# Attention of a two-layer encoder trunk rearranged: value projections, the value product, the rotation, the root vector and the order of the projections

## The chip, the cores and the metric

The kernel runs on one core of a Trainium2 chip, in one launch. The metric is the device time of that core in microseconds (us). A measurement of this kernel can tell about 0.2% from no change, which is 2.3 us here.

## What is computed

The input x is 512 tokens by 1024 features, in float32. Each of two layers does the following:

```python
h = rmsnorm(x, attn_norm[l])
proj = h @ w_in[l]                        # 1024 -> 3072: sb_q, sb_k, sb_v, df_q, df_k, df_v, 512 columns each
# stick-breaking group: 8 heads of 64, causal and strict
z = q @ k.T / 8
w = exp(log_sigmoid(z) + sum of log_sigmoid(-z) over the keys between), 0 where key >= query
sb_out = w @ v
# differential group: 4 heads with two score maps of 64 and values of 128
dq, dk = rope(df_q), rope(df_k)
p = softmax(dq @ dk.T / 8)                # a query sees the keys of its own and of earlier chunks of 64 tokens
df_out = rmsnorm((p[0] - lam * p[1]) @ dv, subln_norm[l]) * (1 - lambda_init)
x = x + concat(sb_out, df_out) @ w_o[l]
# dense part
x = x + square(relu(rmsnorm(x, mlp_norm[l]) @ w_ff1[l])) @ w_ff2[l]
```

After the second layer comes a last rmsnorm. The result is float32.

## The kernel before

**Number format.** A float32 product is made of three TensorE products. Each operand is split into a high part (`hi`, rounded by ScalarE as it copies into the format fp32r) and the rest (`lo`, a VectorE subtraction). `three` (L278) issues hi*hi, hi*lo and lo*hi into the same PSUM bank; they are lines L281, L282 and L283 of the profile. Weights are split in the kernel too: `_Weights` (L86) loads a raw block of 128 x 1024 by a transfer of SyncE's queue (L99), and splits it on ScalarE (L116, tile `whi`) and VectorE (L117, tile `wlo`). A block is split when the block before it starts to be used, so its split has about one block of TensorE work to be done in.

**Projections.** x is held with features on the 128 partitions and the 512 tokens along the free axis. A projection block (`block`, L291) is 128 columns of w_in: the weights are the stationary operand, h is the moving one, eight chunks of features by three products of 512 columns, 24 matmuls. Its result has the projected columns on the partitions. The root of the norm differs from token to token. It is not yet known when the first blocks run, so h leaves it out, and it is multiplied in at the eviction: `rms_a` (L244) transposes the sums of squares, reduces them and raises them to -1/2 on GpSimd (L259, tile `rcol`, a token on each partition). From this it makes two diagonal matrices (L264, L266), and `rms_b` (L271) multiplies them with a matrix of ones, which spreads the roots along the free axis of every partition (tile `rbc`). The same pair of functions does the norm of each differential head (tiles `rs_d`, `dgh`, `dgl`, `rb_d`).

**Evictions.** A value block (`evict_v`, L367) is multiplied by `rbc` on VectorE (L369), then turned by four TensorE transposes (L374, tile `vT`), since the value product needs keys on the partitions, and then split (L381 on ScalarE, L382 on VectorE). A differential query or key block (`evict_d`, L430) is multiplied by cosine and by sine on VectorE (L433, L434). GpSimd then forms the two sums of the rotation (L441, L442), 3.5 us of the planner's clock later the result is split, and twelve transfers (L408) on SyncE's queue lay it out in the stacks `st` and `kl` from which the scores are made.

**Attention.** A unit is half of the queries (256) of one head. Three stages run at a lag: scores and weights (`s1_df` L488, `s1_sb` L468), transposes of the weights in 128 x 128 pieces (`s2` L542, transposes at L555, split at L224 and L225 into `zh`, `zl`, `fh`, `fl`), and the value product (`s3` L572, matmuls at L583 and L584 for stick-breaking heads and at L281 to L283 for differential ones, bank `O`). For the first half of the queries `s3` multiplies two key blocks, for the second half four, all of 256 columns, with a strip of zeros where a key block is later than the queries. That is six matmuls of 256 columns for each kind of product and head. There are two kinds of product for a stick-breaking head, three for a differential one.

**Order of the work.** TensorE takes its instructions in program order. `dense` (L698) walks `ORDER` (L31): d is a pair of differential query and key blocks, w a differential value block, s and u the same for stick-breaking heads. Then comes the first half of the output projection, `wo(1)`. After each matmul triple of this, the planner adds attention steps, at a rate that spreads the attention's planned cost (`ATT`) over the planned dense time (`DENSE`), all but the last `TAIL` of it. A unit may start when the planned clock says that its stacks are laid out. The second half, `wo(0)`, follows, and then the dense part of the layer. The framework then orders each engine's instructions by its own estimate of when they can start.

**PSUM.** Eight banks: two "t" (transposes), two "mm" (projections), three "s" (scores), one "o" (value product). A block can start when its bank has been evicted.

Of the kernel before, what the change touches and what calls it, by code (L numbers as in the profile page):

```python
# [9 lines left out]
F32 = mybir.dt.float32  # L10
# [7 lines left out]
P = 128  # L18
S = 512
# [15 lines left out]
RST = 2  # L35
WARM = 10
RA, RB, DLY_V = (21, 20), (32, 31), 3.5
# [3 lines left out]
TAIL, ATT, DENSE, CAP = 6.0, 54.0, 145.0, 0.1  # L41
# [8 lines left out]
def _unit_list():  # L50
# [5 lines left out]
    for l in range(L):  # L56
        for item in ORDER:
            b = int(item[1])
            if item[0] == "d":
                units.append(("x", l, b, 0))  # L60
                units.append(("x", l, b, 1))
            elif item[0] == "s":
                qk(l, SBQ, SBK, b)
            else:
                units.append(("p", l, (SBV if item[0] == "u" else DFV) + b * P))
# [86 lines left out]
def trunk(ctx, tc, xT, w, w2, gains, gfin, lamv, cos, sin, out):  # L152
# [23 lines left out]
    rbc = cp.tile([P, S], F32, tag="rbc", name="rbc")  # L176
# [19 lines left out]
    ones = cp.tile([P, 1], F32, tag="ones", name="ones")  # L196
    nc.vector.memset(ones, 1.0)
# [18 lines left out]
    chi = cp.tile([P, 4], F32R, tag="chi", name="chi")  # L216
    clo = cp.tile([P, 4], F32, tag="clo", name="clo")
    ones_r = cp.tile([P, 1], F32R, tag="onesr", name="ones_r")
    nc.vector.memset(ones_r.bitcast(F32), 1.0)
    fin = cp.tile([P, 24], F32, tag="fin", name="fin")  # L220
    cp.tile([P, 88], F32, tag="trail", name="trail")
# [22 lines left out]
    def rms_a(src, inv_n, col, name, eng, dgt, floor=None):  # L244
        pt = bank("t", "rs_" + name)
        if RST and eng is not nc.gpsimd or RST == 2:
            for j in range(4):
                nc.tensor.transpose(pt[:, j * P : (j + 1) * P], src[:, j * P : (j + 1) * P], ident)
            nc.vector.tensor_reduce(out=ms, in_=pt.rearrange("p (j f) -> p j f", j=4), axis=AX.X, op=ALU.add)
            if floor is None:  # L250
                nc.vector.tensor_scalar(out=ms, in0=ms, scalar1=inv_n, scalar2=EPS, op0=ALU.mult, op1=ALU.add)
            else:
                nc.vector.scalar_tensor_tensor(
                    out=ms, in0=ms, scalar=inv_n, in1=floor, op0=ALU.mult, op1=ALU.add)
        else:
            for j in range(4):
                nc.tensor.matmul(pt[:, j : j + 1], src[:, j * P : (j + 1) * P], ones, start=True, stop=True)
            nc.vector.tensor_scalar(out=ms, in0=pt[:, 0:4], scalar1=inv_n, scalar2=EPS, op0=ALU.mult, op1=ALU.add)
# [3 lines left out]
        dg_hi, dg_lo = dgt("dgh" + name), dgt("dgl" + name)  # L262
        idb = ident.unsqueeze(1).to_broadcast([P, 4, P])
        eng.tensor_mul(  # L264
            dg_hi.rearrange("p (j t) -> p j t", j=4), idb, chi.bitcast(F32).unsqueeze(2).to_broadcast([P, 4, P]))
        eng.tensor_mul(  # L266
            dg_lo.rearrange("p (j t) -> p j t", j=4), idb, clo.unsqueeze(2).to_broadcast([P, 4, P]))

        return dg_hi, dg_lo
# [47 lines left out]
    for l in range(L):  # L317
        with ExitStack() as actx:
# [9 lines left out]
            zt = []  # L328
            for i in range(2):
                zh = ap_.tile([P, 512], F32R, tag=f"zh{i}", name=f"zh{l}_{i}")  # L330
# [779 lines left out]
```

## Time and profile before

| | |
|---|---|
| median of 3 runs | 1173.92 us (1173.44 to 1175.14) |
| the profiled execution: its span, first to last instruction | 1173.7 us |
| TensorE busy, matmuls | 1149.1 us, 98% of the span, 5454 matmuls |
| VectorE busy | 817.8 us, 70% |
| ScalarE busy | 651.7 us, 56% |
| GpSimd busy | 213.7 us, 18% |
| transfers | 170.11 MB, mean 145 GB/s |

No separate time is given for the profiled execution; its span lies 0.2 us under the median of the runs. The page names the engine, the line of the kernel, the operation and the tiles (`out<-in`). A matmul's recorded duration overlaps the next one, so what a matmul costs is read from the distance of two starts, in a timeline of TensorE. The attention and its projections take the stretches from 8 to 231 us and from 583 to 803 us; the dense parts of the layers run from 254 to 574 us and from 836 us on.

### The profile page before, as it was taken

To read this page: it belongs to the slowest core of one execution; us is meant where nothing else is said; L and a number is where in the kernel's file an instruction comes from. 1 tells how busy PE (TensorE), PEld (TensorE's weight loads), DVE (VectorE), ACT (ScalarE), POOL (GpSimd) and SP (SyncE) were. 2 spreads that over 40 slices of the span, in tenths; PEclk is the share of its full clock that TensorE was granted. 3 is DMA by queue.
4 is the path that set the end of the run, shared out by engine and by line. 5 is a ranking of instruction groups with operands and counts; after the bars stand their busy time and mean duration, and the time that the engine had idled before them with its cause. 6 is when DMAs were issued, how large, how long until landed. Compare 5 with 4: busy or idle time off the path is not lost.

```text
span 1173.7 us, 15335 instructions
## 1 busy us (share of the span) xinstructions
PE 1149.1 (98%) x5454; PEld 952.0 (81%) x5454; DVE 817.8 (70%) x1301; ACT 651.7 (56%) x1153; POOL 213.7 (18%) x283
## 2 busy tenths in 40 slices
PE   9999999999999999999899999999999999999995
PEld 6887888888888888888677888888888888888884
DVE  7888788785546747646878887877665466476567
ACT  6455666556656456455445556655666563554545
POOL 1221442130101101002012215331201010010022
PEclk9999999999999999999999999999999999999999
DMA  7645433245844836737416553432558357276184
GB/s 245 174 138 170 127 108 111 70 179 163 210 139 113 220 126 125 223 94 160 100 55 189 153 161 108 129 105 72 220 122 231 122 124 222 97 172 192 33 170 129
DMA packets 56860, 170.11 MB, mean 145 GB/s; under 512 B 7120, under 2 KB 8144, under 8 KB 56784
## 3 DMA queue, kind: packets, MB, share of 16 engines
q1 hardware_dynamic: 46416, 131.88, 33.7%
q0 software_dynamic: 10224, 37.23, 17.9%
q8 instruction: 43, 0.70, 0.2%
q14 instruction: 33, 0.27, 0.1%
q10 hardware_dynamic: 144, 0.02, 0.0%
HBM read 138.17 MB, written 2.10 MB: 120 GB/s over the span
## 4 chain that ended last, share of the span: by engine, by line
PE 84%; DVE 6%; DMA 3%; issue 2%; ACT 1%; POOL 1%; SPq 0%; POOLq 0%; DVEq 0%; ACTq 0%
PE f L282 10%; PE f L281 10%; PE f L283 10%; PE x L282 4%; PE x L281 4%; PE x L283 4%; PE wo L281 2%; PE wo L282 2%; PE wo L283 2%; DMA q<-in_w 2%; DVE wlo L117 1%; PE T0s L555 1%; PE T1s L555 1%; ACT whi L116 1%; DVE h_lo L229 1%
## 5 line engine op out<-in xcount | busy, mean ns | idle before, releaser
L117 DVE TENSOR_TENSOR wlo<-raw,whi 128x1024 fp32r<-128x1024 f32 (+1 forms) x132 | 158.0, 1201 | 95.9 <-ACT whi L116 95.0
L117 DVE TENSOR_TENSOR wlo<-q,whi 128x512 fp32r<-128x512 f32 x224 | 146.2, 688 | 106.0 <-ACT whi L116 105.6
L281 PE MATMUL f<-h_hi,whi 128*128 128x512 f32 x512 | 199.6, 390 | 0.0
L283 PE MATMUL f<-h_hi,wlo 128*128 128x512 f32 x512 | 199.2, 389 | 0.0
L282 PE MATMUL f<-h_lo,whi 128*128 128x512 f32 x512 | 199.2, 389 | 0.0
L116 ACT ACTIVATE whi<-q 128x512 fp32r<-128x512 f32 x224 | 129.5, 624 | 120.1 <-DMA q<-in_w 39.1
L116 ACT ACTIVATE whi<-raw 128x1024 fp32r<-128x1024 f32 (+1 forms) x132 | 133.9, 1019 | 111.0 <-PE f L282 54.5
L783 POOL DMA_DIRECT2D q<-in_w x64 | 55.9, 873 | 556.8 <-DVE wlo L117 471.4
L283 PEld LDWEIGHTS f<-h_hi,wlo 128*128 128x128 f32 x512 | 96.1, 188 | 20.0
L281 PEld LDWEIGHTS f<-h_hi,whi 128*128 128x128 f32 x512 | 96.1, 188 | 19.9
L282 PEld LDWEIGHTS f<-h_lo,whi 128*128 128x128 f32 x512 | 96.1, 188 | 19.7
L225 DVE TENSOR_TENSOR Al<-F,Ah 128x256 fp32r<-128x256 f32 (+2 forms) x96 | 74.8, 779 | 44.1 <-ACT Ah L224 44.0
L281 PE MATMUL x<-whi,Ah 128*128 128x512 f32 x256 | 100.2, 392 | 0.0
L282 PE MATMUL x<-wlo,Ah 128*128 128x512 f32 x256 | 99.7, 390 | 0.0
L283 PE MATMUL x<-whi,Al 128*128 128x512 f32 x256 | 99.7, 389 | 0.0
L224 ACT ACTIVATE Ah<-F 128x256 fp32r<-128x256 f32 (+2 forms) x96 | 67.6, 704 | 45.7 <-DVE F L819 43.7
L282 PEld LDWEIGHTS x<-wlo,Ah 128*128 128x128 f32 x256 | 48.1, 188 | 10.0 <-DVE wlo L117 0.4
L283 PEld LDWEIGHTS x<-whi,Al 128*128 128x128 f32 x256 | 48.0, 188 | 10.0
L281 PEld LDWEIGHTS x<-whi,Ah 128*128 128x128 f32 x256 | 48.1, 188 | 9.8
L810 ACT ACTIVATE F<-f 128x512 f32<-128x512 f32 x64 | 37.5, 587 | 9.9 <-DVE Al L225 5.5
L811 ACT ACTIVATE F<-F 128x512 f32<-128x512 f32 x64 | 40.3, 630 | 1.5
L228 ACT ACTIVATE h_hi<-x,g_all 128x512 fp32r<-128x512 f32 x32 | 22.6, 720 | 30.6 <-DVE x L692 17.5
(1060 smaller groups left out, 2574.6 us busy)
## 6 DMA issues: line engine op xcount, KB each, us to landing
raw<-in_w SPq DMA_DIRECT2D x126, 512.0 KB, 3.6
q<-in_w SPq DMA_DIRECT2D x64, 512.0 KB, 5.3
q<-in_w POOLq DMA_DIRECT2D x64, 512.0 KB, 5.7
x<-in_xT SPq DMA_DIRECT2D x8, 256.0 KB, 4.1
raw<-in_w SPq DMA_DIRECT2D x8, 128.0 KB, 4.1
yx<-y POOLq DMA_DIRECT2D x2, 512.0 KB, 8.8
y<-y POOLq DMA_DIRECT2D x2, 512.0 KB, 7.5
y<-yx POOLq DMA_DIRECT2D x2, 512.0 KB, 5.2
```

Of the source, the lines that this page charges most:

```text
L116: h = nc.scalar.activation(hi[:, a:b], raw[:, a:b], AF.Copy)
L117: self.last = h, nc.vector.tensor_tensor(out=lo[:, a:b], in0=raw[:, a:b], in1=hi[:, a:b].bitcast(F32), op=ALU.subtract)
L224: nc.scalar.activation(hi, src, AF.Copy)
L225: nc.vector.tensor_tensor(out=lo, in0=src, in1=hi.bitcast(F32), op=ALU.subtract)
L228: a = nc.scalar.activation(h_hi[:, c, :], x[:, c, :], AF.Copy, scale=g)
L281: nc.tensor.matmul(pt, ah, bh, start=first, stop=False)
L282: nc.tensor.matmul(pt, ah, bl, start=False, stop=False)
L283: nc.tensor.matmul(pt, al, bh, start=False, stop=last)
L555: nc.tensor.transpose(pt[:, off : off + P], u["w"][qi][:, kb * P : (kb + 1) * P], ident)
L783: nc.gpsimd.dma_start(t, quad(g, q, c), accum_op=ALU.add)
L810: nc.scalar.activation(t, pt, AF.Relu)
L811: nc.scalar.activation(t, t, AF.Square)
```

## The change

- **Values.** `values` replaces the value blocks: h is now the stationary operand and two blocks of value weights (256 columns) are the moving one, so the result has tokens on the partitions and needs no transpose. Four token blocks by eight chunks by three products of 256 columns are 96 matmuls for two value blocks. They are collected in two PSUM banks. The root is a scale for each partition there (`rcol`), applied in the eviction: ScalarE makes hi, VectorE lo, four pieces of 256 columns each.
- **Value product.** `s3` has no step for the first half of the queries. At the second half it does all four: key block 0 with 512 query columns, key block 1 with 384, key block 2 with 256, key block 3 with 128. The zero strips are gone, and the turned weights of both halves stay in one pair of tiles (`zh`, `zl`).
- **Rotation.** The two sums are made by VectorE right behind the multiplications.
- **Roots.** `rms_a` ends with the column of roots, and `rms_b` transposes each of the four columns, repeated 128 times, in place of the two diagonal matrices and the two matmuls.
- **Order.** d0 d1 w0 d2 d3 s0 w1 s1 u0 s2 s3 u1, where w and u are now pairs of value blocks. There are four general tiles in place of five (`TB`), `rbc` shares the tile `ssq`, and the planner's numbers are 52.3 for the attention and 147.5 for the dense time.

```diff
+M256 = 0.114
-ORDER = ("d0", "w0", "d1", "w1", "d2", "w2", "d3", "w3", "s0", "u0", "s1", "u1", "s2", "u2", "s3", "u3")
+ORDER = ("d0", "d1", "w0", "d2", "d3", "s0", "w1", "s1", "u0", "s2", "s3", "u1")
-TB = 5
+TB = 4
-TAIL, ATT, DENSE, CAP = 6.0, 54.0, 145.0, 0.1
+TAIL, ATT, DENSE, CAP = 6.0, 52.3, 147.5, 0.1
...
-    rbc = cp.tile([P, S], F32, tag="rbc", name="rbc")
+    rbc = ssq
...
         nc.gpsimd.tensor_tensor(out=col, in0=ms, in1=mhalf, op=ALU.pow)
-        nc.vector.tensor_copy(chi, col)
-        nc.vector.tensor_sub(clo, col, chi.bitcast(F32))
...
-    def rms_b(bc, name, dg, tag="t"):
-        dg_hi, dg_lo = dg
+        return col
+
+    def rms_b(bc, name, col, tag="t"):
         pb = bank(tag, "rb_" + name)
-        nc.tensor.matmul(pb, ones_r.to_broadcast([P, P]), dg_hi, start=True, stop=False)
-        nc.tensor.matmul(pb, ones_r.to_broadcast([P, P]), dg_lo, start=False, stop=True)
+        for j in range(4):
+            nc.tensor.transpose(pb[:, j * P : (j + 1) * P], col[:, j : j + 1].to_broadcast([P, P]), ident)
         nc.scalar.copy(bc, pb)
...
-            def evict_v(pt, kind, b, which):
-                t = tt(f"tv{l}{kind}{b}")
-                nc.vector.tensor_mul(t, pt, rbc)
-
-                def rest():
-                    tv = bank("s" if kind == "u" else "t", f"vT{l}{kind}{b}")
+            def values(kind, pr, tags):
+                pts = [bank(tag, f"v{l}{kind}{pr}{i}") for i, tag in enumerate(tags)]
+                for half in range(2):
+                    u = W.next("v")
                     for tb in range(4):
-                        nc.tensor.transpose(tv[:, tb * P : (tb + 1) * P], t[:, tb * P : (tb + 1) * P], ident)
+                        pt = pts[tb // 2]
+                        to = pt[:, tb % 2 * 256 : tb % 2 * 256 + 256]
+                        hs = slice(tb * P, tb * P + P)
+                        for c in range(4):
+                            k = 4 * half + c
+                            three(to, (h_hi[:, k, hs], h_lo[:, k, hs]), wpair(u, c, 256),
+                                  k == 0 and tb % 2 == 0, k == KC - 1 and tb % 2 == 1)
+                            yield 3 * M256
+                        if half == 1 and tb % 2 == 1:
+                            evict_v(pt, kind, pr, tb - 1)
...
+                    r = rcol[:, tb : tb + 1]
+                    nc.scalar.activation(hi, src, AF.Copy, scale=r)
+                    nc.vector.scalar_tensor_tensor(
+                        out=lo, in0=src, scalar=r, in1=hi.bitcast(F32), op0=ALU.mult, op1=ALU.subtract)
...
                 u1, v1 = heads.pop(("x", b))
+                nc.vector.tensor_sub(u1, u1, v)
+                nc.vector.tensor_add(v1, v1, u)
 
                 def rest():
-                    nc.gpsimd.tensor_sub(u1, u1, v)
-                    nc.gpsimd.tensor_add(v1, v1, u)
...
             def s3(u):
                 half, b, m, kind = u["half"], u["b"], u["m"], u["kind"]
                 key = (kind, b, m)
                 if half == 0:
-                    heads[key] = bank("o", f"O{l}{kind}{b}{m}")
-                o = heads[key][:, half * 256 : half * 256 + 256]
-                n = 2 * half + 2
-                for kb in range(n):
-                    wh, wl = u["wT"][kb]
+                    return
+                o = bank("o", f"O{l}{kind}{b}{m}")
+                z = turned.pop(key)
...
+                for kb in range(4):
+                    if kb == 0:
+                        to, (wh, wl) = o.rearrange("p (r c) -> p r c", r=2), (wide(t) for t in z)
+                    else:
+                        a, e = ((256, 640), (896, 1152), (1152, 1280))[kb - 1]
+                        to, (wh, wl) = o[:, kb * P : 512], (t[:, a:e] for t in z)
...
+                    if kind in "wu":
+                        for cost in values(kind, b, ("s", "mm") if step == 32 else ("mm", "mm")):
+                            yield cost
+                        step += 16
+                        continue
```

**What moves in the order.** In the rows below an instruction has its line (of the kernel before or of the changed one, which differ), its operation, the tile it writes, the tiles it reads and the size of what it writes.

First place: TensorE in layer 0, at the start of the scores of the last differential head. `p0s0q` is a stick-breaking query block (layer 0, pair 0), `vT0w` a transposed value block, `S0d` a score bank, `st0d3` and `kl0d3` the stacks of differential head 3, `v0w` the new value banks. The projection of head 3, `p0d3k`, ends 66 rows ahead of the first score row shown for the kernel before, and 101 rows ahead of it in the changed one. Before:

```order
L374 MATMUL vT0w_1080<-edge,tv0w_1053 128x128 x4
L281 MATMUL p0s0q<-h_hi,whi_961 128x512
L282 MATMUL p0s0q<-h_lo,whi_961 128x512
L283 MATMUL p0s0q<-h_hi,wlo_962 128x512
L465 MATMUL S0d_1092<-st0d3k,st0d3q 128x256
```

TensorE at the same scores in the changed kernel, now inside the second pair of value blocks:

```order
L262 MATMUL v0w_1052<-whi_955,h_lo 128x256
L260 MATMUL v0w_1052<-whi_955,h_hi 128x256
L261 MATMUL v0w_1052<-wlo_956,h_hi 128x256
L262 MATMUL v0w_1052<-whi_955,h_lo 128x256
L445 MATMUL S0d_1087<-st0d3k,st0d3q 128x256
```

The transposes of the values are gone, the value matmuls have 256 columns, and the scores of head 3 stand a whole pair of query and key blocks later than its projection.

Second place: VectorE in layer 1, behind the roots. `cos_t` takes the spread roots in (tile `rbc`, now `ssq`), `u1d0q` to `v1d1q` are the products with cosine and sine of differential heads 0 and 1, `wlo` the split of a weight block, `hl1d0k` the split of a rotated head. Before:

```order
L719 TENSOR_TENSOR cos_t<-cos_t,rbc 128x512
L720 TENSOR_TENSOR sin_t<-sin_t,rbc 128x512
L433 TENSOR_TENSOR u1d0q<-p_5294,cos_t 128x512
L434 TENSOR_TENSOR v1d0q<-p_5294,sin_t 128x512
L433 TENSOR_TENSOR u1d0k<-p_5295,cos_t 128x512
L434 TENSOR_TENSOR v1d0k<-p_5295,sin_t 128x512
L369 TENSOR_TENSOR tv1w_5524<-p1w0v,rbc 128x512
L433 TENSOR_TENSOR u1d1q<-p1d1q,cos_t 128x512
L434 TENSOR_TENSOR v1d1q<-p1d1q,sin_t 128x512
L117 TENSOR_TENSOR wlo_5532<-raw_5439,whi_5531 128x1024
L225 TENSOR_TENSOR hl1d0k<-u1d0q,hl1d0k 128x512
```

VectorE in the changed kernel from `cos_t` on; the weight block `wlo_5588` is the second half of the first pair of values:

```order
L696 TENSOR_TENSOR cos_t<-cos_t,ssq 128x512
L697 TENSOR_TENSOR sin_t<-sin_t,ssq 128x512
L413 TENSOR_TENSOR u1d0q<-p_5355,cos_t 128x512
L414 TENSOR_TENSOR v1d0q<-p_5355,sin_t 128x512
L413 TENSOR_TENSOR u1d0k<-p_5356,cos_t 128x512
L414 TENSOR_TENSOR v1d0k<-p_5356,sin_t 128x512
L420 TENSOR_TENSOR v1d0q<-v1d0q,u1d0k 128x512
L419 TENSOR_TENSOR u1d0q<-u1d0q,v1d0k 128x512
L413 TENSOR_TENSOR u1d1q<-p1d1q,cos_t 128x512
L414 TENSOR_TENSOR v1d1q<-p1d1q,sin_t 128x512
L118 TENSOR_TENSOR wlo_5588<-raw_5492,whi_5587 128x1024
L220 TENSOR_TENSOR hl1d0k<-u1d0q,hl1d0k 128x512
```

The two sums of the rotation stand in VectorE's row now, the multiplication of a value block by the roots is gone from it, and the weight split is the eleventh instruction from `cos_t` on, where it was the tenth.

Third place: TensorE in layer 0, where the attention ends. `O0s` is the value product of the last stick-breaking head, `wo` with `mdh` the end of the first half of the output projection, `wo` with `vdh` the start of the second half, which reads the heads' results. Before:

```order
L282 MATMUL wo_2541<-mdl_142,whi_2443 128x512
L283 MATMUL wo_2541<-mdh_141,wlo_2444 128x512
L583 MATMUL O0s_2554<-zh_1_150,vs_143 128x256
L584 MATMUL O0s_2554<-zl_1_151,vs_143 128x256
L583 MATMUL O0s_2554<-zh_1_150,vs_143 128x256
L584 MATMUL O0s_2554<-zl_1_151,vs_143 128x256
L281 MATMUL wo_2579<-mdh_141,whi_2443 128x512
L282 MATMUL wo_2579<-mdl_142,whi_2443 128x512
L283 MATMUL wo_2579<-mdh_141,wlo_2444 128x512
```

Nine more `wo` rows with `mdh` follow there before the first one with `vdh`. TensorE at the same place in the changed kernel, from the last transposes of the head's weights (`T0s`) on:

```order
L533 MATMUL T0s_2630<-edge,sig0s_2555 128x128 x2
L260 MATMUL wo_2607<-mdh_134,whi_2489 128x512
L261 MATMUL wo_2607<-mdl_135,whi_2489 128x512
L262 MATMUL wo_2607<-mdh_134,wlo_2490 128x512
L557 MATMUL O0s_2640<-zh0s_2582,vs_136 128x512
L558 MATMUL O0s_2640<-zl0s_2583,vs_136 128x512
L557 MATMUL O0s_2640<-zh0s_2582,vs_136 128x384
L558 MATMUL O0s_2640<-zl0s_2583,vs_136 128x384
L557 MATMUL O0s_2640<-zh0s_2582,vs_136 128x256
L558 MATMUL O0s_2640<-zl0s_2583,vs_136 128x256
L557 MATMUL O0s_2640<-zh0s_2582,vs_136 128x128
L558 MATMUL O0s_2640<-zl0s_2583,vs_136 128x128
```

The first row with `vdh` follows directly. The last value product has moved behind all of the first half of the output projection, 12 matmuls later than before.

More of the change, by code (lines that the diff above doesn't have):

```diff
@@ new lines, in s3 @@
+                if kind == "s":
+                    if m == 0:
+                        heads[("mt", b)] = a2.tile([P, S], F32, tag="mt", name=f"mt{l}{b}", bufs=MTB)
+                    mt = heads[("mt", b)]
+                    oc = tt(f"oc{l}{b}{m}")[0:64, :]
+                    nc.scalar.copy(oc, o[64:128, :])
+                    nc.vector.tensor_add(mt[64 * m : 64 * m + 64, :], o[0:64, :], oc)
+                    if m == 1:
+                        split(ms_hi[:, b, :], ms_lo[:, b, :], mt)
+                else:
+                    os_ = a2.tile([P, S], F32, tag="mt", name=f"os{l}{b}", bufs=MTB)
+                    sqo = tt(f"sqo{l}{b}")
+                    nc.scalar.activation(sqo, o, AF.Square)
+                    nc.scalar.activation(os_, o, AF.Copy, scale=gsub[:, l : l + 1])
+                    rc = a3.tile([P, 4], F32, tag="rc", name=f"rc{l}{b}")
+                    late.append((b, os_, sqo, rc))
```

153 lines of the change are left out of this document (49 added, 104 removed).

## The prediction

> **What bounds the kernel now.** I read the page first: busy times, then the chain that ended last.
>
> ```profile
> PE 1149.1 (98%) x5454; PEld 952.0 (81%) x5454; DVE 817.8 (70%) x1301; ACT 651.7 (56%) x1153; POOL 213.7 (18%) x283
> PE 84%; DVE 6%; DMA 3%; issue 2%; ACT 1%; POOL 1%; SPq 0%; POOLq 0%; DVEq 0%; ACTq 0%
> ```
>
> TensorE is busy for 98% of the span and holds 84% of the chain. So the time changes by what TensorE no longer does, or does in addition, and by its waits. A share over the whole run doesn't say in which stage it waits. The windows do (columns: length, then busy time of PE, PEld, DVE, ACT and POOL, the granted clock, the share and rate of the transfers).
>
> ```profile
> 28.00:50.00 22.00, 21.39 (x100) 17.05 (x100) 18.93 (x32) 7.99 (x18) 6.05 (x4) 1.00 0.52 138
> 50.00:100.00 50.00, 48.24 (x250) 39.83 (x250) 44.59 (x102) 26.88 (x63) 10.01 (x7) 1.00 0.58 174
> 100.00:200.00 100.00, 100.00 (x556) 85.37 (x555) 80.15 (x131) 63.45 (x135) 39.26 (x65) 1.00 0.41 127
> 254.00:574.00 320.00, 319.97 (x1413) 264.78 (x1414) 193.32 (x282) 176.61 (x275) 30.68 (x35) 1.00 0.61 161
> 596.00:680.00 84.00, 79.44 (x390) 64.64 (x389) 69.78 (x142) 38.97 (x86) 16.85 (x16) 1.00 0.52 151
> 680.00:803.00 123.00, 123.00 (x689) 105.10 (x688) 99.38 (x156) 78.31 (x163) 44.65 (x75) 1.00 0.38 116
> ```
>
> In the later attention (100 to 200, 680 to 803) TensorE never waits. Only the first part of each layer has gaps: 0.61 + 1.76 + 4.56 = 6.9 us. VectorE is near its limit there (44.59 of 50 us). The granted clock is 1.00 in all these rows. The dense window gives the price of a 512-column matmul: 319.97/1413 = 0.2265 us. TensorE's waits name the gaps (total, times, longest):
>
> ```profile
> PE p1d2q L281 <- ACT whi L116: 1.4, 1, 1.4
> PE S1d L465 <- DMA kl1d3k<-hl1d3k: 1.4, 1, 1.4
> PE S0d L465 <- issue: 1.3, 1, 1.3
> PE p1w0v L283 <- DVE wlo L117: 0.9, 1, 0.9
> PE p0d2q L283 <- DVE wlo L117: 0.6, 1, 0.6
> PE S1d L465 <- DMA st1d0q<-hl1d0k: 0.4, 1, 0.4
> PE T0d L555 <- DVE p0d L532: 0.4, 1, 0.4
> ```
>
> **What the other matmuls cost.** TensorE's timeline (start, recorded duration) gives distances of starts.
>
> ```profile
> 144.10 0.60 PE L374 MATMUL vT0u<-edge,tv0u 128*128 128x128 f32 x4
> 144.46 0.48 PE L465 MATMUL S0s<-st0s0k,st0s0q 128*128 128x512 f32 x1
> 144.77 0.39 PE L466 MATMUL S0s<-kl0s0k,st0s0q 128*128 128x512 f32 x1
> 152.92 0.40 PE L283 MATMUL p0s2k<-h_hi,wlo 128*128 128x512 f32 x1
> 153.15 0.28 PE L583 MATMUL O0s<-fh0s,vs 128*128 128x256 f32 x1
> 153.27 0.28 PE L584 MATMUL O0s<-fl0s,vs 128*128 128x256 f32 x1
> 153.39 0.28 PE L583 MATMUL O0s<-fh0s,vs 128*128 128x256 f32 x1
> 153.51 0.28 PE L584 MATMUL O0s<-fl0s,vs 128*128 128x256 f32 x1
> 153.62 0.40 PE L281 MATMUL p0s2k<-h_hi,whi 128*128 128x512 f32 x1
> ...
> 155.49 0.33 PE L465 MATMUL S0s<-st0s1k,st0s1q 128*128 128x384 f32 x1
> 155.66 0.34 PE L466 MATMUL S0s<-kl0s1k,st0s1q 128*128 128x384 f32 x1
> 155.84 0.40 PE L281 MATMUL p0s2k<-h_hi,whi 128*128 128x512 f32 x1
> ```
>
> Four of 256 columns take 153.62 - 153.15 = 0.47, so 0.1175 each. 384 columns take (155.84 - 155.49)/2 = 0.175. Four transposes and one 512 take 144.77 - 144.10 = 0.67; less 0.23 that is 0.44, or 0.11 for one transpose.
>
> **TensorE's work, part by part.**
>
> (a) Values: 16 blocks of 24 matmuls, 384 of 512 columns, become 8 pairs of 96, 768 of 256. That is 768 x 0.1175 - 384 x 0.2265 = 90.2 - 87.0 = **+3.3**. Rounding in the rows (0.115 to 0.119) makes it +1.3 to +4.4.
>
> (b) Sixteen groups of value transposes go: -16 x 0.44 = **-7.0**.
>
> (c) The roots are spread ten times, once for the attention's norm and once for each of four heads, in two layers. Two matmuls of 512 columns (0.45) become four transposes (0.44): **-0.1**.
>
> (d) The value product: a kind of product for one head costs 6 x 0.1175 = 0.705 now. It becomes 0.2265 + 0.175 + 0.1175 + x, with x for 128 columns in this format, which no row shows. The line through 512 and 256 columns gives x = 0.063; a transpose, also 128 columns with a weight load of its own, has 0.11; a floor at the full 0.2265 of a 512 is the far end. I take 0.11, the nearest row. There are 2 layers x (4 heads x 3 + 8 heads x 2) = 56: 56 x (0.629 - 0.705) = **-4.3**, with ends of -6.9 and +2.3. The Trainium skill ("TensorE: Matmul & The Clock Gate", Back-to-back issue gap) gives about 81 ns for 128 columns in a stream of load and matmul pairs; by that estimate (d) would be 1.6 us lower. It also gives 131 ns for 512, where this trace has 226.5, so I go by the rows.
>
> Together (a) to (d): 3.3 - 7.0 - 0.1 - 4.3 = **-8.1 us** of TensorE.
>
> **The waits.** Head 3's scores (first place of the order) wait 1.3 and 1.4 us now. Its key block and first scores stand in the trace as
>
> ```profile
> L283 PE MATMUL p0d3k<-h_hi,wlo x8: 389/389/397, 73.7 to 81.4; 128*128 128x512 f32 x8
> L465 PE MATMUL S0d<-st0d3k,st0d3q x8: 274/347/389, 96.7 to 113.5; 128*128 128x256 f32 x4, 128*128 128x384 f32 x2, 128*128 128x512 f32 x2
> ```
>
> so layout takes up to 96.7 - 81.4 = 15.3 us from the end of the projection. In the new order 101 rows lie between, holding 55 matmuls of 512 columns, 7 of 384, 26 of 256 and 17 short ones: 12.5 + 1.2 + 3.1 + 1.9 = 18.6 us. The stacks are then laid out with 3 us to spare, and both waits go: -2.7. The rotation's move to VectorE takes one step of GpSimd out of this chain as well. The next late thing would be the first heads' stacks, and there the 0.4 of `st1d0q` stays.
>
> `p0d2q` (0.6) now comes behind a pair of values, 96 x 0.1175 = 11.3 us in which VectorE makes two weight splits; I drop the wait, and the 0.4 of `T0d` too, which came from VectorE's queue. At the second place VectorE reaches the second value block's split late:
>
> ```profile
> 610.62 0.69 DVE L719 TENSOR_TENSOR cos_t<-cos_t,rbc 128x512 f32<-128x512 f32 x1 [3.58 <-ACT rbc L276]
> 611.23 0.68 DVE L720 TENSOR_TENSOR sin_t<-sin_t,rbc 128x512 f32<-128x512 f32 x1
> 616.98 1.22 DVE L117 TENSOR_TENSOR wlo<-raw,whi 128x1024 fp32r<-128x1024 f32 x1
> ```
>
> A step of VectorE is 611.23 - 610.62 = 0.6 us. Ten of them and the split of 1.22 are 7.2 us from `cos_t` on. TensorE, which is released by the same roots, has 48 value matmuls and a triple of 512 in that time, 5.6 + 0.7 = 6.3. That is a wait of 0.9 and a hand-over; I take 1.3, in place of the 1.4 of `p1d2q`. Behind that split stand the splits of head 0 and with them its stacks; layer 1's entry wait of 0.9 stays, for another tile.
>
> At the third place the last value product has moved behind the output projection's first half. Its results go through
>
> ```profile
> 224.11 0.58 ACT L597 COPY oc<-O0s 64x512 f32<-64x512 f32 x1 [3.01 <-PE O0s L584]
> ...
> 225.45 0.63 ACT L224 ACTIVATE vdh<-mt 128x512 fp32r<-128x512 f32 x1 [0.75 <-DVE mt L598]
> ```
>
> ```profile
> 224.73 0.69 DVE L598 TENSOR_TENSOR mt<-O0s,oc 64x512 f32<-64x512 f32 x1 [0.40 <-ACT oc L597]
> 226.11 0.69 DVE L225 TENSOR_TENSOR vdl<-mt,vdh 128x512 fp32r<-128x512 f32 x1 [0.70 <-ACT vdh L224]
> L225 DVE TENSOR_TENSOR zl<-T0s,zh 128x384 fp32r<-128x384 f32 x16 | 8.6, 539 | 0.2 <-ACT zh L224 0.2
> ```
>
> From `oc`'s start to `vdl`'s end these are 226.80 - 224.11 = 2.7 us. Ahead of the first matmul that needs them stand 9 to 12 of other heads, 2.0 to 2.7 us. And between the last transposes and this product only one triple (0.7) covers the split, whose low half alone takes 0.54. Between 0 and 1.7 us a layer are exposed; I take 0.75, so **+1.5**.
>
> Waits together: -1.3 - 1.4 - 0.6 - 0.4 - 0.1 + 1.5 = **-2.3**, with ends of -5 (nothing new waits) and +4 (the old ones stay, tail and second place at their worst).
>
> **VectorE.** It loses 16 multiplications of value blocks, 16 low splits and four diagonal matrices, and gains 16 rotation sums and 32 low pieces of 256 columns:
>
> ```profile
> L819 DVE SCALAR_TENSOR_TENSOR F<-F 128x256 f32<-128x256 f32 x64 | 26.9, 421 | 0.8
> ```
>
> 32 x 0.42 + 16 x 0.6 - 36 x 0.6 = 13.4 + 9.6 - 21.6 = +1.4 us over both layers, less some tiny copies. I cost that at nothing: from 100 us on, VectorE has 20% free and TensorE doesn't wait. If that cover is gone (the first part of a layer) it is in the ends of the waits. A pair's eviction frees its first bank while the other bank's 48 matmuls run in two halves, 24 x 0.1175 = 2.8 us behind it, more than two pieces (0.84) take; it costs nothing as long as VectorE isn't late. GpSimd only loses work.
>
> **Sum.** -8.1 - 2.3 = -10.4 against the execution's span of 1173.7, or 1163.3; the median of 1173.92 lies 0.2 above that execution, so **1163.5 us**. About 0.2%, 2.3 us, is what a measurement of this kernel can tell from no change.
>
> **The rivals.**
>
> 1. The matmuls get cheaper, but the waits don't fall: another stack or split is late where head 3's was. For it: VectorE at 90% there, and two heads projected back to back at a layer's start. Against: 3 us to spare. 1173.9 - 8.1 = 1165.8. Chance 0.10.
> 2. A matmul of 128 columns costs as much as one of 512. No row shows one in this format. 56 x (0.2265 - 0.11) = +6.5: 1170.0. Against it: the transposes. Chance 0.12.
> 3. A pair of values holds two banks where a block held one, so it starts only when both are evicted. VectorE evicts heads just ahead of pairs with four to six steps of 0.6. If each of 8 pairs waits for two steps, 8 x 1.2 = 9.6 and the gain is gone: 1173.1, no change. Against: the second bank is needed 2.8 us after the first. Chance 0.09.
> 4. Slower. The values become unbroken runs of up to 96 matmuls of 256 columns, each with its own weight load; now such matmuls come in groups of four to eight between wider ones. A load is recorded longer than that:
>
> ```profile
> L283 PEld LDWEIGHTS f<-h_hi,wlo 128*128 128x128 f32 x512 | 96.1, 188 | 20.0
> ```
>
> If in a long run the wide neighbours no longer lend their time, each matmul costs its load's 188 ns: 768 x (0.188 - 0.1175) = +54 us, 1217.6. It decides from 10.4/768 = 13.5 ns on, that is from 0.131 us a matmul. Against it: in the rows above four in a row keep 0.1175 with a load each, and a queue that ran dry would show in the fourth. The Trainium skill ("TensorE: Matmul & The Clock Gate", Part 3: Packing small matmuls) says that a weight load overlaps matmuls in flight only when the row groups differ, and here every load uses all rows. By that rule this rival would hold from the first matmul on; the four at 0.1175, under their loads' 188 ns, disagree. Chance 0.07.
>
> **How the numbers follow.** The forecast has 0.62. Its own ends: -2.0 in (a), -2.6 in (d) and -2.7 in the waits below, of which I grant about two thirds at once: 1158.5; above, waits of +4 more, 1167.5. Up to 1170.5 rivals 1 and 2 lie inside. Outside are rivals 3 and 4 (0.16) and 0.04 of the forecast's tails. Faster by over 0.2%: 0.62 + 0.10 + 0.12 = 0.84. Rival 3 is within 0.2% with 0.07 of its chance, and slower with 0.02, which makes 0.09 with rival 4.
>
> **What would show it.** In the profile after, value matmuls should start 0.115 to 0.12 apart (at 0.13 and more, rival 4), matmuls of 128 columns 0.06 to 0.11 apart (rival 2: 0.2 or more). TensorE's busy time should fall by about 8. `S0d` and `S1d` should be gone from its waits for heads 3, `p0d2q` too; a wait of a second block in the first pair of layer 1 should be there with about 1.3, and waits of `O` or `wo` at the attention's end with under 1 a layer. A wait of value banks for VectorE would be rival 3. I am wrong if TensorE's busy time falls by under 5 us, or its waits grow.

## The result and the profile after

| | before | after |
|---|---|---|
| median | 1174.09 us (1173.44 to 1175.14, 4 runs) | 1163.43 us (1163.37 to 1164.68, 4 runs) |
| ratio | | 0.9916, 95% interval 0.9902 to 0.9930 |
| the profiled execution: span | 1173.7 us | 1162.8 us |
| its time | | 1164.68 us |

The kernel is faster by 0.84%, 10.7 us by the medians. In two later runs (after_again and rot_only) the profiled execution had a granted clock of 0.85; the comparisons leave such executions out, and their profiles are not read here.

The page of the changed kernel, busy times and chain:

```profile
PE 1142.8 (98%) x5682; PEld 961.8 (83%) x5682; DVE 799.1 (69%) x1291; ACT 656.1 (56%) x1169; POOL 174.7 (15%) x243
PE 88%; DVE 5%; DMA 2%; ACT 2%; issue 1%; POOL 1%; POOLq 0%; ACTq 0%; DVEq 0%
```

TensorE is busy for 6.3 us less, with 228 matmuls more, and holds more of the chain. Its idle time fell from 1173.7 - 1149.1 = 24.6 to 20.0 us, by 4.6. The windows of the changed kernel show where (length, then busy time of PE, PEld, DVE, ACT, POOL):

```profile
28.00:50.00 22.00, 22.00 (x149) 20.24 (x148) 17.75 (x33) 9.29 (x19) 0.00 (x0) 1.00 0.55 149
50.00:100.00 50.00, 49.23 (x287) 42.63 (x285) 45.38 (x114) 28.92 (x74) 2.31 (x2) 1.00 0.70 198
100.00:200.00 100.00, 99.33 (x623) 88.62 (x622) 76.73 (x118) 64.64 (x135) 32.95 (x59) 1.00 0.38 115
596.00:680.00 84.00, 83.04 (x499) 73.22 (x498) 69.57 (x159) 43.19 (x101) 3.53 (x4) 1.00 0.62 179
680.00:803.00 123.00, 122.31 (x731) 106.93 (x730) 94.88 (x138) 75.95 (x155) 37.86 (x68) 1.00 0.35 103
```

The first part of the attention waits for 0.77 + 0.96 us where it waited for 6.9 (layer 1 now stands some 5 us earlier, so the last two windows hold a little more of it). The later part, which had no gap, has one of 0.7 in each layer. TensorE's waits in the attention name them:

```profile
PE p1d2q L260 <- ACT whi L117: 1.0, 1, 1.0
PE p1d1q L262 <- DVE wlo L118: 0.9, 1, 0.9
PE S0d L445 <- DMA st0d2q<-hl0d2k: 0.8, 1, 0.8
PE T0s L533 <- DVE zl0d L220: 0.6, 1, 0.6
PE T1s L533 <- DVE zl1d L220: 0.6, 1, 0.6
```

With one of 0.2 more these are 4.1 us; the list of before, with its 0.2, has 6.6. The difference of 2.5 is close to the forecast's 2.3, but it is made of other rows: the two waits of head 3's scores and that of `p0d2q` are gone as foreseen, and head 2's scores and the transposes of the first stick-breaking head wait instead. The rest of the idle time that went (4.6 - 2.5) lies outside of this list: `rs_m`, the next norm's transposes at the attention's end, waited for 0.7 before and doesn't now, and the waits of `xT` and `yT` at the ends of the layers' dense parts came to 6.4 before and 5.2 after. The change doesn't touch those dense parts, and over the traces of the experiments, which don't either, the same waits come to between 3.6 and 6.0.

TensorE's timeline gives the prices. First a stretch of a pair of values:

```profile
33.91 0.28 PE L262 MATMUL v0w<-whi,h_lo 128*128 128x256 f32 x1
34.03 0.28 PE L260 MATMUL v0w<-whi,h_hi 128*128 128x256 f32 x1
...
35.35 0.28 PE L262 MATMUL v0w<-whi,h_lo 128*128 128x256 f32 x1
```

Twelve matmuls lie between the first row and the last: 1.44/12 = 0.120 each, in the middle of an unbroken run. Then the end of a value product, where 128 columns appear:

```profile
220.95 0.28 PE L557 MATMUL O0s<-zh0s,vs 128*128 128x256 f32 x1
221.06 0.28 PE L558 MATMUL O0s<-zl0s,vs 128*128 128x256 f32 x1
221.18 0.22 PE L557 MATMUL O0s<-zh0s,vs 128*128 128x128 f32 x1
221.24 0.27 PE L558 MATMUL O0s<-zl0s,vs 128*128 128x128 f32 x1
221.35 0.45 PE L260 MATMUL wo<-vdh,whi 128*128 128x512 f32 x1
221.64 0.39 PE L261 MATMUL wo<-vdl,whi 128*128 128x512 f32 x1
```

The first of 128 columns takes 0.06, the second 0.11. But the 512 behind them takes 221.64 - 221.35 = 0.29, where one in the same stretch takes 0.23: what the first narrow matmul saves is paid behind the last. All 24 heads show it, with 0.055 to 0.062 for the first narrow one, and behind the last 0.28 to 0.29 for a 512 or 0.17 for a 256, 0.05 to 0.06 too much (one of them waits as well). Transposes do the same: in the prediction's rows, the 512 behind four of them takes 144.77 - 144.46 = 0.31. So a price has to take in this stretched matmul. Adding up the distances of the starts over all value products gives 40.0 us before and 34.7 after; with the 1.3 us in the stretched matmuls behind them it is 36.0 after.

### The profile page after: what moved, and what is told of

Same layout as the page of the kernel before. It is cut to its first block, busy times and chain, and to the rows that moved or that the text cites. A ratio compares the mean times of both kernels' runs of the same rounds, so it can differ in the third digit from the quotient of the medians.

```text
span 1162.8 us, 15712 instructions
## 1 busy us (share of the span) xinstructions
PE 1142.8 (98%) x5682; PEld 961.8 (83%) x5682; DVE 799.1 (69%) x1291; ACT 656.1 (56%) x1169; POOL 174.7 (15%) x243
## 4 chain that ended last, share of the span: by engine, by line
PE 88%; DVE 5%; DMA 2%; ACT 2%; issue 1%; POOL 1%; POOLq 0%; ACTq 0%; DVEq 0%
PE f L260 10%; PE f L261 10%; PE f L262 10%; PE x L261 4%; PE x L262 4%; PE x L260 4%; PE wo L260 3%; PE wo L261 3%; PE wo L262 3%; DVE wlo L118 1%; PE T1s L533 1%; PE T0s L533 1%; DMA q<-in_w 1%; DMA y<-y 1%; PE v0w L260 1%
## 5 line engine op out<-in xcount | busy, mean ns | idle before, releaser
L787 ACT ACTIVATE F<-f 128x512 f32<-128x512 f32 x64 | 37.5, 587 | 10.9 <-DVE Al L220 5.5
```

The source lines that it names most:

```text
L787: nc.scalar.activation(t, pt, AF.Relu)
```

## The experiments

All are changes to the changed kernel but rot_only, which changes the kernel before. Ratios are to the kernel before, on the same chip; the changed kernel itself had 0.9916, and 0.9895 when it ran again.

**The same kernel again.** 

> The changed kernel once more, unchanged, beside the three others of this set, so that they have it on the same chip. Every theory expects 0.9916 of the kernel before, within 0.2%.

Measured: 1162.31 us, 0.9895 (0.9882 to 0.9909). So two measurements of one kernel lie 0.2% apart, and single differences of under 2 us say nothing here.

### The value product

**old_widths.** The edit:

```diff
-                    if kb == 0:
-                        to, (wh, wl) = o.rearrange("p (r c) -> p r c", r=2), (wide(t) for t in z)
-                    else:
-                        a, e = ((256, 640), (896, 1152), (1152, 1280))[kb - 1]
-                        to, (wh, wl) = o[:, kb * P : 512], (t[:, a:e] for t in z)
+                runs = (((0, 0), (256, 640)), ((0, 128), (256, 384)), ((256, 896),), ((256, 1024),))
+                    for n, (at, c0) in enumerate(runs[kb]):
+                        to, (wh, wl) = o[:, at : at + 256], (t[:, c0 : c0 + 256] for t in z)
```

> The changed kernel with the value product in six matmuls of 256 columns again for each kind of product and head, in place of 512, 384, 256 and 128; two of the six take other columns than the kernel before did, which doesn't alter their number. Theory (TensorE's work sets the time): 56 x (6 x 0.1195 - 0.61) = +6.0 by the distances in the trace of the changed kernel, +4.3 by the forecast's 0.11 for the narrow one: 1167.7 to 1169.4. Rival (the end of the attention is set by VectorE and ScalarE, and TensorE's saving there is given back): under +1.5, 1165 or less.

Measured: 1166.53 us, 0.9930 (0.9917 to 0.9943). Against the two ratios of the changed kernel that is 2 to 4 us more. It lies between the rival's 1165 and the theory's 1167.7, so the time alone doesn't decide. In the trace the value products take 40.05 us again, and no narrow one stretches what stands behind: 4.0 more than the 36.0 of the changed kernel. Of this, 0.8 comes back because the wait of head 2's scores isn't there, and 0.6 because `T0s` and `T1s` wait for 0.3 in place of 0.6. At the attention's end, where the rival looked, the matmuls that stand out in the changed kernel (223.48, below) take 0.2 less a layer, 0.4 together. So the widths are worth TensorE's 4 us, less what the waits shift, and the rival holds for 0.4 of it.

**narrow_times4.** The edit:

```diff
+                    for rep in range(4 if kb == 3 else 1):
                         if kind == "s":
```

> The changed kernel with each product of 128 columns issued four times in place of once (the fourth key block's share of the value product then counts fourfold): 168 more such matmuls. It measures their price. At the forecast's 0.11 each: +18.5, 1182; at 0.06, the distance of two narrow ones in a row in the trace of the changed kernel: +10.1, 1173.5; at the mean of 0.085 that a pair has there: +14.3, 1177.7; at a 512's 0.2265, the rival of the prediction: +38, 1201.

Measured: 1184.14 us, 1.0085 (1.0071 to 1.0099); 21.8 us more than the changed kernel beside it. The value products take 53.5 us in place of 34.7, so 18.8/168 = 0.112 each; of the rest, waits account for some 2 us (head 2's scores in layer 1 wait for 1.0, for one). TensorE's timeline of this kernel shows that 0.06 doesn't last:

```profile
152.64 0.22 PE L559 MATMUL O0s<-zh0s,vs 128*128 128x128 f32 x1
152.69 0.28 PE L560 MATMUL O0s<-zl0s,vs 128*128 128x128 f32 x1
152.81 0.28 PE L559 MATMUL O0s<-zh0s,vs 128*128 128x128 f32 x1
...
153.37 0.28 PE L560 MATMUL O0s<-zl0s,vs 128*128 128x128 f32 x1
153.48 0.44 PE L260 MATMUL p0s2k<-h_hi,whi 128*128 128x512 f32 x1
153.76 0.40 PE L261 MATMUL p0s2k<-h_lo,whi 128*128 128x512 f32 x1
```

Only the first is short. From the second on they start (153.37 - 152.69)/6 = 0.113 apart, and the transposes, also with 128 columns and a load each, had 0.11. The 512 behind the row takes 0.28 in place of 0.23, as behind a pair, so the added matmuls are charged at their full price. The forecast's 0.11 holds for each narrow matmul, and the rival with a 512's price is refuted.

### The value blocks

**old_values.** The value blocks of before (blocks of 24 matmuls, `evict_v` with its multiplication, transposes and split) in the order `d0 d1 w0 w1 d2 d3 s0 w2 w3 s1 u0 u1 s2 s3 u2 u3`.

> The changed kernel with the value blocks of before (24 matmuls of 512 columns, a multiplication, four transposes and a split for each), two blocks where the pair stood. Theory: 384 x 0.2265 + 16 x 0.44 - 768 x 0.120 = 87.0 + 7.0 - 92.2 = +1.9 of TensorE by the trace of the changed kernel (+3.7 by the forecast), and no new waits: 1165 to 1167.5. Rival (the values' rework takes waits of VectorE away, which is where most of the gain is): +5 or more, 1168.5 and over. Other rival (the transposes are hidden): no change, 1163.4.

Measured: 1172.03 us, 0.9975 (0.9962 to 0.9988): 7 to 9 us more, which the theory doesn't allow. One wait stands out in this kernel's list, which the changed kernel doesn't have:

```profile
PE rs_m L888 <- POOL ssq L232: 3.4, 2, 2.0
```

It is the next norm's, at the attention's end. The planner still had 147.5 for a dense time that is 145.2 by its own prices with the value blocks of before, and 1.52 us of attention were left over in place of 0.76.

**old_values_plan.** So the same with one number of the plan:

```diff
-TAIL, ATT, DENSE, CAP = 6.0, 52.3, 147.5, 0.1
+TAIL, ATT, DENSE, CAP = 6.0, 52.3, 144.0, 0.1
```

> The value blocks of before in the changed kernel again, now with the planned dense time set to 144.0, so that the attention ends as in the changed kernel (0.76 us of it left over, in place of 1.52). Theory (the values' rework is worth TensorE's 1.3 to 1.9 us, and the rest of the 6.9 us of the first try came from the plan, which ended late and let the next norm wait 3.4 us for GpSimd): 1165 to 1166.5, and no wait of the norm's transposes. Rival (the values' rework itself frees VectorE and GpSimd at the end of the attention): 1168.5 or more, with that wait still there.

Measured: 1167.89 us, 0.9936 (0.9924 to 0.9948). The norm's wait is gone, and 4 to 5 us with it, so the plan was worth that much. The time lies between the theory (up to 1166.5) and the rival (1168.5 or more). By the distances of starts, without idle time and with each stretched matmul's surplus counted to the transposes ahead of it, the value blocks take 88.7 us here and their 64 transposes 6.1 + 1.2, together 96.0; the pairs take 92.4 in the changed kernel. On TensorE the rework of the values is worth 3.6, where the forecast has 7.0 - 3.3 = 3.7. The median says 4.8 more than the changed kernel of the same set. The profiled execution was the fastest of its six (1165.10, the others up to 1168.92), and waits for less at the ends of the dense parts (3.6 in place of 5.2), so what the median has beyond TensorE's 3.6 isn't in a trace.

### The order and the rotation

**order_w1_early.**

```diff
-ORDER = ("d0", "d1", "w0", "d2", "d3", "s0", "w1", "s1", "u0", "s2", "s3", "u1")
+ORDER = ("d0", "d1", "w0", "d2", "w1", "d3", "s0", "u0", "s1", "s2", "u1", "s3")
```

> The changed kernel with the order d0 d1 w0 d2 w1 d3 s0 u0 s1 s2 u1 s3, so that head 3's projection stands nearer to its scores again. Theory (the order took 2.7 us of score waits away): those of head 3 come back, 1.3 us a layer, 1165.5 to 1166.5; TensorE's busy time stays. Rival (the order is worth nothing, the planner fills in other matmuls until the stacks are there): 1163 to 1164 and no wait for head 3.

Measured: 1166.66 us, 0.9933 (0.9918 to 0.9948), 2 to 4 us more against the two ratios of the changed kernel. TensorE's waits in this kernel:

```profile
PE S0d L445 <- DMA st0d2q<-hl0d2k: 2.0, 1, 2.0
...
PE rs_m L906 <- POOL ssq L233: 1.1, 2, 0.7
PE S1d L445 <- DMA kl1d2k<-hl1d2k: 1.0, 1, 1.0
```

The size was about right, the place wrong: head 2 waits, not head 3, and the attention's end slips too. Head 2's projection stands at the same place in both orders, and the trace doesn't say why its scores wait longer here. Head 3's projection ends 12.5 us ahead of its first score, nearer than the 14.8 of the kernel before, and still they don't wait: its last transfer is issued 10.1 us behind the projection, where it was 14.0 before. So the order matters to the time, but this run doesn't show that the distance alone took head 3's waits away.

**rot_gpsimd.**

```diff
-                nc.vector.tensor_sub(u1, u1, v)
-                nc.vector.tensor_add(v1, v1, u)
 
                 def rest():
+                    nc.gpsimd.tensor_sub(u1, u1, v)
+                    nc.gpsimd.tensor_add(v1, v1, u)
```

> The changed kernel (1163.4 us) with the two sums of the rotation back on GpSimd, behind the 3.5 us of the planner's clock. Theory (the gain is TensorE's own work, 7 to 8 us, and the rest is the order's waits): the rotation is worth within 1.5 us either way, 1162 to 1165; the wait of 1.0 for the weight block in layer 1's first pair of values gets shorter, since VectorE reaches that split two steps of 0.6 earlier, and stacks come about 2 us later. Rival (VectorE's rotation, by earlier stacks, is a large part of the gain): 1166.5 or more, with score waits of 3 us more.

Measured: 1167.66 us, 0.9947 (0.9928 to 0.9965): 4 to 6 us more, so my theory of a neutral rotation falls. The rival has the time, but not its 3 us of score waits: `S0d` waits for 1.0 in all. VectorE's timeline in layer 1, behind the roots, shows what the theory missed. In the changed kernel it has

```profile
605.59 0.69 DVE L696 TENSOR_TENSOR cos_t<-cos_t,ssq 128x512 f32<-128x512 f32 x1 [3.72 <-ACT ssq L255]
...
611.59 1.21 DVE L118 TENSOR_TENSOR wlo<-raw,whi 128x1024 fp32r<-128x1024 f32 x1
```

and with the rotation on GpSimd

```profile
606.94 0.69 DVE L696 TENSOR_TENSOR cos_t<-cos_t,ssq 128x512 f32<-128x512 f32 x1 [3.72 <-ACT ssq L255]
...
611.57 0.69 DVE L413 TENSOR_TENSOR u1d1q<-p1d1q,cos_t 128x512 f32<-128x512 f32 x1 [0.94 <-POOL v1d0q L422]
612.83 0.69 DVE L414 TENSOR_TENSOR v1d1q<-p1d1q,sin_t 128x512 f32<-128x512 f32 x1 [0.56 <-POOL u1d0q L421]
613.44 1.22 DVE L118 TENSOR_TENSOR wlo<-raw,whi 128x1024 fp32r<-128x1024 f32 x1
...
616.97 1.99 DVE L118 TENSOR_TENSOR wlo<-raw,whi 128x1024 fp32r<-128x1024 f32 x1
```

VectorE has two instructions less, but waits for 0.94 and 0.56 until GpSimd releases a general tile, of which there are four. The split starts 6.5 us behind the cosines instead of 6.0, and TensorE waits for it for 1.7. The next block's split, beside GpSimd's next sum, takes 1.99 in place of 1.22. Only then come the stacks, for which the scores wait here (0.7 for head 0 in layer 0).

**rot_only.** The kernel before with this part alone (`sub` and `add` of the rotation on VectorE, five general tiles).

> The kernel before (1174.1) with one part of the change alone: the two sums of the rotation on VectorE, right behind the multiplications. It has five general tiles, as before. Theory from the trace of the changed kernel with the rotation on GpSimd (VectorE waited 0.94 and 0.56 there for tiles that GpSimd still held, and its instructions beside GpSimd took 1.78 and 1.99 in place of 0.68 and 1.22): the rotation alone brings 2 to 3 us, 1171 to 1172, and the score waits of 1.3 and 1.4 get shorter. Rival (it is worth that only with four tiles): 1173.5 to 1174.5.

Measured: 1171.34 us, 0.9974 (0.9966 to 0.9983). So it brings 3 us (2 to 4) by itself, with five tiles too. Whether the score waits get shorter isn't shown. The waits of VectorE in the kernel before, with its five tiles, already hold

```profile
DVE v1d1q L434 <- POOL u1d0q L441: 0.6, 1, 0.6
DVE v0d1q L434 <- POOL u0d0q L441: 0.6, 1, 0.6
```

and two shorter ones of the same kind (0.3 and 0.2): there too VectorE waits for tiles that GpSimd holds.

### The waits that are left

**stack_delay10.**

```diff
-DLY_R, DLY_D, DLY_S = 3.5, 8.0, 6.0
+DLY_R, DLY_D, DLY_S = 3.5, 10.0, 6.0
```

> The changed kernel with the planner's time for a differential head's stacks at 10.0 in place of 8.0, so that scores are asked for later. Theory (the 0.8 to 1.0 us that head 2's scores wait in layer 0 is a late stack, and other matmuls can fill it): -0.8, 1162.6, and no such wait. Rival (the attention then ends later by as much): 1163.4 or more.

Measured: 1162.68 us, 0.9901 (0.9889 to 0.9913), no difference from the changed kernel. Head 2's wait and those of `T0s` and `T1s` for `zl` are gone. Head 2's query stacks also land in 2.7 to 4.2 us here, where they took 5.3 to 6.3 in the changed kernel, so whether later scores or earlier stacks took its wait away is not shown. This one has come:

```profile
PE wo L260 <- DVE vs L360: 0.9, 2, 0.4
```

**evict_later.** The second place of the order again, with head 1's eviction held back:

```diff
-                            for args in held:
+                            now, held = (held[:2], held[2:]) if step == 32 else (held, [])
+                            for args in now:
...
+                            if n == 3:
+                                for args in held:
+                                    evict_d(*args)
```

> The changed kernel with the eviction of head 1 (two multiplications of its query block) behind the split of the second value block of the first pair, two steps of VectorE later than now. Theory (VectorE's ten steps from the cosines on make that split late, and 1.0 us of TensorE waits there in layer 1): the split ends 1.2 us earlier, the wait goes, -1.0, 1162 with 1163 for the changed kernel, and VectorE's row shows the split 4.8 us behind the cosines in place of 6.0. Rival (ScalarE's split for the next block is late by itself, as the row of the wait names it): the wait stays, no change.

Measured: 1162.80 us, 0.9905 (0.9892 to 0.9918). VectorE's timeline has the split where the theory put it, 4.8 us behind the cosines:

```profile
604.21 0.69 DVE L700 TENSOR_TENSOR cos_t<-cos_t,ssq 128x512 f32<-128x512 f32 x1 [3.72 <-ACT ssq L255]
...
609.01 1.22 DVE L118 TENSOR_TENSOR wlo<-raw,whi 128x1024 fp32r<-128x1024 f32 x1
```

The wait of `p1d2q` is gone, so it was VectorE's steps and not ScalarE that caused it. (Head 2's wait isn't in this list either, and `p1d1q` waits for 1.2 in place of 0.9.) But TensorE's list has a new one, two blocks on:

```profile
PE p1d3q L262 <- DVE wlo L118: 1.0, 1, 1.0
```

**evict_later_delay.** 

> The same, with the planner's time for the stacks at 10.0 as well, which took the wait of head 2's scores away but moved others. Theory: both waits gone, 1161 to 1162, the fastest of all so far. Rival: waits of the value splits at the attention's end (1.2 in two places) come instead, 1163.

Measured: 1163.08 us, 0.9905 (0.9892 to 0.9918). Again no gain that can be told. Both waits are gone, as the theory had it, but `p1d3q` waits for 0.8 and 0.3, and `wo` for 0.9, this for value splits at the attention's end, as the rival had it. Between its 1163 and the theory's 1162 the time can't decide. No version beats the changed kernel by more than can be told.

## Why the prediction was right, point by point

The time came out at 1163.43 for 1163.5, and at 1162.31 when the kernel ran again. The mechanism was right: less work for TensorE, nearly as priced, and shorter waits in the first part of the attention, though the waits only in part for the reasons given. The table sets each term beside the traces of the two kernels. TensorE's terms are distances of starts without idle time, and what a matmul is stretched by transposes or narrow matmuls ahead of it is counted to those.

| term | forecast | before | after | difference |
|---|---|---|---|---|
| (a) values | +3.3 | 89.5 | 92.4 | +2.9 |
| (b) value transposes | -7.0 | 5.6 + 1.4 | 0 | -7.0 |
| (c) roots | -0.1 | 5.0 | 3.5 + 0.8 | -0.6 |
| (d) value product | -4.3 | 40.0 | 34.7 + 1.3 | -4.0 |
| waits in the attention | -2.3 | 6.6 | 4.1 + 0.6 | -1.9 |
| sum | -10.4 | | | -10.6 |

The span fell by 10.9. Two things that the forecast didn't have make up the rest: the waits of `rs_m`, `xT` and `yT` are 2 us shorter, and matmuls that the change doesn't touch take nearly 2 us more (1.3 of it in the dense parts' second product, tile `x`). That these two cancel is luck. The second one is also why TensorE's busy time fell by 6.3 only, where the prediction had about 8; its cause is not shown.

- **(a) Values, +3.3.** Right, by two prices that were both too low. In the long runs 256 columns take 0.120 (92.4/768), not 0.1175; the 512s of the value blocks took 89.5/384 = 0.233, not the 0.2265 of the dense part. That the groups were short was rival 4's reason; its mechanism, loads that the neighbours no longer hide, is refuted, since the run above holds 0.120 under recorded loads of 188 ns. The rule of the Trainium skill that I set beside it ("TensorE: Matmul & The Clock Gate", Part 3: Packing small matmuls: a load overlaps only a matmul of another row group) would have put the starts at least a load, 0.188, apart; the trace disagrees.
- **(b) Value transposes, -7.0.** Right. In the kernel before, the 64 transposes take 5.6 us by distances of starts, and the matmuls behind the groups are stretched by 1.4 in all.
- **(c) Roots, -0.1.** The spreading took 5.0 us before and 3.5 after by distances of starts, some 0.3 of it a wait; the stretched matmuls behind the ten groups of transposes give 0.8 back. Not tested alone.
- **(d) Value product, -4.3.** Right, with the step "I take 0.11, the nearest row": a narrow matmul costs 0.112 in a row (narrow_times4), and in a pair the 0.06 of the first is made up by 0.06 in the matmul behind the second. Read without that matmul, the trace seems to say 0.085 and -5.3. The estimate of the Trainium skill (81 ns, "TensorE: Matmul & The Clock Gate", Back-to-back issue gap) lies below the 0.112 measured, and its 131 ns for 512 columns doesn't fit either trace.
- **The waits, -2.3.** Right in sum (-2.5 in the list, +0.6 at the tail, so -1.9), and half right in kind. Head 3's scores wait no longer: in layer 0 its last transfer lands at 86.2 and the first score starts at 89.3, the 3 us to spare that were forecast. Whether the order did this is open, since head 3 doesn't wait in order_w1_early either. The 0.4 of `st1d0q`, which was to stay, is gone. The second place waits for 1.0, where I had 1.3, and for the reason given; the row names ScalarE because TensorE's order has two matmuls of `p1d2q` ahead of the late split. The tail was over-priced: +0.75 a layer, while in TensorE's timeline there only two matmuls stand out,

```profile
223.48 0.92 PE L260 MATMUL wo<-vdh,whi 128*128 128x512 f32 x2
224.23 0.40 PE L261 MATMUL wo<-vdl,whi 128*128 128x512 f32 x1
```

which take 0.75 in place of 0.45, 0.3 a layer. What the step left out is what came new: head 2's scores (0.8), and the bank of `T0s` and `T1s` (0.6 each). VectorE's timeline shows why the bank is held: the split that frees it (`zl0d`, two pieces) stands behind a long scan of the next head:

```profile
124.26 1.22 DVE L463 TENSOR_TENSOR_SCAN C0s<-keep0s,edge 128x512 f32<-128x512 f32 x1
125.39 1.12 DVE L220 TENSOR_TENSOR zl0d<-T0d,zh0d 128x512 fp32r<-128x512 f32 x2
```

- **The rotation.** I priced it at nothing but a shorter chain. It is worth about 3 us in the kernel before (rot_only) and 4 to 6 in the changed one (rot_gpsimd), and the order is worth 2 to 4 (order_w1_early). What the step left out are VectorE's waits for tiles that GpSimd holds. Undone alone, each of the two brings waits, but neither brings those of head 3 back, so which of them took these away stays open. The sum was right because it counted the waits, not because it knew their cause.
- **VectorE, +1.4, priced at nothing.** The parts that were named come to that (+1.5 in the trace), but VectorE's busy time fell from 817.8 to 799.1. The "tiny copies" of the roots (`chi`, `clo`) took 7.7 us, and other instructions got shorter, `sm0d` and `sm1d` (L529, L509) from 12.4 to 6.6, `h_lo` from 27.8 to 23.7. TensorE's time doesn't show this as a term of its own.
- **The sum.** The 0.2 between the execution and the median compares a span with a time. In the changed kernel the profiled execution's time is 1.9 above its span (1164.68 and 1162.8). The forecast isn't touched by it: 1173.92 - 10.4 is 1163.5 as well.
- **The rivals.** Rival 1 (waits that take the old ones' place) is half true, as the new rows show. Rival 2 and rival 4 are refuted by the prices above. No wait for a value bank is in the list, so rival 3 falls as well.

The undone parts add up to 2 to 4 (widths), 5 (values), 4 to 6 (rotation) and 2 to 4 (order), more than the 11 that all bring. Each leaves the plan and the tile counts of the others as they are; that this is the reason is not shown.

## What to carry to other kernels

On a kernel whose one engine is busy for 98% of the time, the sum of start-to-start distances is a good forecast, but take each from a run of the length that the new code will have (0.1175 in a group of four was 0.120 in a run), and measure up to the matmul behind the group: the 0.06 of one narrow matmul was paid back there, and its price was 0.112. Moving a short elementwise step to the busier engine can pay when the slower one holds buffers that the busier one waits for. Waits that one edit removed returned one block on here (evict_later); look for what stands next in the same queue before counting them as gained.

## What the runs showed of the hardware

- Matmuls of 128 columns that each load new weights settle at 0.112 us, half of a 512's 0.2265 for a quarter of its columns. The first behind a wider one takes 0.06, and the wider one behind the last takes 0.05 to 0.06 more than otherwise (0.28 to 0.29 in place of 0.23 for 512 columns).
- A matmul of 256 columns holds 0.120 with a load of its own each time, 0.008 above a narrow one's 0.112.
- VectorE's split of a 128x1024 block took 1.99 us beside a GpSimd sum in rot_gpsimd; those of that run with no GpSimd instruction beside them took 1.20 to 1.23.
- Head 3's query stacks in layer 0 of the changed kernel land 2.7 to 2.9 us after their issue; head 2's took twice that there, and 2.7 to 4.2 in stack_delay10. What held them is not shown:

```profile
L388 SPq DMA_DIRECT2D st0d2q<-hl0d2k x4: 537/568/1234, 64.9 to 69.0; - x4
...
DMA to landing us min/median/max: 5.3/5.7/6.3
```
